# Seven products for eight in a second output projection, and a different block order at its end

## The chip, the cores and the metric

The kernel runs on one core of one Trainium2 chip. The metric is the device time of one execution in microseconds (us). The engines of the core are named as in the profile: PE is TensorE (matrix multiply), PEld its weight loads, DVE is VectorE, ACT is ScalarE, POOL is GpSimd, SP is SyncE, which here only issues DMAs.

## What is computed

Two layers of a decoder trunk work on 256 tokens of 2048 features, in float32. Cut to what matters here:

```
for layer in range(2):
    attn = moba_attention(h, ...) or swa_attention(h, ...)   # ends in  o @ w_o   (256x2048 @ 2048x2048)
    h = layer_norm(ALPHA * h + attn, ln_g[layer, 0], ln_b[layer, 0])
    ffn = conv_ffn(h, w_up, conv_w, conv_b, w_down)          # 2048 -> 2 x 5504 -> 2048
    h = layer_norm(ALPHA * h + ffn, ln_g[layer, 1], ln_b[layer, 1])
```

The change is about `o @ w_o`, the output projection of the attention. "Layer 1" in the title of the change is the first layer, which the code numbers 0; from here on the code's numbers are used, layer 0 and layer 1.

## The kernel before

**Halves.** All weights come through one stream of *halves*: a half is a 128 x 1024 piece (512 KB), that is two weight blocks of 128 rows (`k`) by 512 columns (a *chunk*, `c`). SP issues its load into one of seven `raw` buffers (L143). ACT copies it into the high part `wh` (L162), and DVE subtracts to get the low part `wl` (L171). A product of a data block with a weight block is three matmuls: high by high, high by low, low by high (L386 to L388, or L615 to L617). `take()` hands out the next half and first lets ACT and DVE split three halves further ahead, or more where `reach` says so: near the end of a projection the halves of the next stage go into tiles that have come free (`settle`, `aside`), and the two engines run far ahead of PE.

**Order.** Nothing is scheduled by a tool; the order is that of the program. `step()` counts halves, and `at(n, f)` puts an action `n` steps ahead into an agenda. Each engine works its own instructions in that order, so an action which DVE was given after a split waits for that split, and the split for its weights' DMA.

**The output projection** (`project_out`) has four chunks of 16 blocks. Without quads (layer 0), each chunk has two accumulators, one for each half of the tokens, and after it `fold` adds them to the residual `res` (L521 the first time, L511 later). With quads (layer 1), `two_chunks` does chunks 0 and 1 together: a *quad* is a pair of blocks `2p, 2p+1` in both chunks. Its eight products (two blocks, two chunks, two token tiles) become seven, as in Strassen's scheme. For that it needs sums of weight blocks, made ahead of time in DRAM (the tensors `t`, two halves for each quad, `sum_weights`), and sums of data blocks (`pair_sums`, made by `sum_heads` during the attention). The seven products go into eight accumulator banks; when the quads are done, `chain` combines four of them and `fold` adds the results to `res`.

**Weight sums.** `plan_sums` puts five DMAs for each quad into the agenda: two copies of the plain blocks from DRAM to DRAM on SP (L300), and on POOL one accumulating DMA (L302) and two more (L304, L306), each of which waits for the one before it. The quads of `w_down` (the down projection) are made in the same way during attention and up projection.

**Bias tables.** `spread_bias` writes the relative-position bias of four heads from `ud` to `band` in DRAM; for layer 1 that is on POOL (L317), four DMAs, read by the attention of layer 1 much later.

The order of halves in the two chunks is written out by `wo_halves`: first `WO_LEAD`, then sums (`t`) and plain halves in turn, and at the end `WO_LAST`, two halves of four blocks: blocks 14 and 15 of chunk 0, and then the same of chunk 1.

Of the kernel before, what the change touches and what calls it, by code (L numbers as in the profile page):

```python
# [11 lines left out]
F32 = mybir.dt.float32  # L12
# [5 lines left out]
P = 128  # L18
T = 256
D = 2048  # L20
KB = D // P
NH = 16
# [3 lines left out]
FT = DFF // P  # L26
# [24 lines left out]
TWO_ORDER = [(k, c) for k in range(12) for c in range(2)] + [(k, c) for c in range(2) for k in range(12, KB)]  # L51


QUADS = ((10, 8, 0), (10, 8, 4))
DENSE = ((False, True), (False, False))
LEAD = (4, 2)
WO_LEAD = [(k, 0) for k in range(8, 14)] + [(k, 1) for k in range(8, 12)]
WO_LAST = [(k, c) for c in range(2) for k in (14, 15)]
S_EARLY = 8
QUAD_ORDER = ((0, 1, 2, 3, 4, 5, 8, 9, 6, 7), (0, 1, 2, 3, 4, 5, 6, 7))  # L60
QUAD_LIST = [(l, n, p) for l in range(2) for n in range(3) for p in range(QUADS[l][n])]


def quad_halves(l, n):
# [19 lines left out]
def wo_halves(l):  # L84


    q = range(QUADS[l][2])
    mid = [b for p in q for b in ((2 * p, 0), (2 * p + 1, 0), (2 * p + 1, 1))]
    mid[3:3] = [(12, 1)]
    mid[10:10] = [(13, 1)]  # L90
    halves = lambda bs: [("w", *bs[i:i + 2]) for i in range(0, len(bs), 2)]
    order = halves(WO_LEAD)
    sums, others = [("t", p, i) for p in q for i in range(2)], halves(mid)
    while sums:
        order += [sums.pop(0)] + others[:1]
        others = others[1:]
    return order + others + halves(WO_LAST)

# [6 lines left out]
def trunk(ctx: ExitStack, tc: tile.TileContext, wst, wq, xT_in, x_in, relb, onehot, umask, sinks, conv_in, ln_g, ln_b, out):  # L105
# [114 lines left out]
    def load_input(pool, tables):  # L220
        xc = pool.tile([P, KB, T], F32, name="xc", bufs=1)

        def load_x(k, n=2, queue=nc.sync):
            queue.dma_start(xc[:, k:k + n], xT_in[:, k:k + n, :])

        def split_x(k, n=2):
            ks = slice(k, k + n)
            nc.scalar.activation(xT[:, ks, 0:T], xc[:, ks], AF.Copy)  # L228
            nc.vector.tensor_tensor(out=xT[:, ks, T:2 * T], in0=xc[:, ks], in1=xT[:, ks, 0:T].bitcast(F32),
                                    op=ALU.subtract)  # L230

        load_weights(lambda j: load_x(j, 1, nc.scalar))
        for u in range(1, RAW_FIRST):
            load_weights()
            if u < 3:
                load_x(u + 1, 1)
        load_x(4)
        load_x(6)
        tables()
        split_upto(0, lambda j: split_x(j, 1))  # L240
        for u in range(1, 3):
            split_upto(u)
            split_x(u + 1, 1)
        for k in range(4, KB, 2):
            if k > 6:
                at(k - 7, load_x, k)
            at(k - 3, split_x, k)
        for i in range(RAW_BUFS - RAW_FIRST):
            at(16 + 3 * i, load_weights)

    def load_residual(t):
        nc.sync.dma_start(res[:, t, :], x_in[t * P:(t + 1) * P, :])
# [55 lines left out]
    def plan_sums(quads, n0, step):  # L308


        for j, q in enumerate(quads):
            for i, m in enumerate((0, 2, 5, step + 1, step + 4)):
                at(n0 + j * step + m, sum_weights, q, i)

    def spread_bias(l, h0, h1):
        a = ud[l, h0:h1, :]
# [539 lines left out]
    def layer_attention(l, rest, stage, turnover):  # L856
        oT = st
        kept = []
        if l:
            norm, turned = rest  # L860
            turn, low = turned
            n0 = nexth["i"]
            c = COLS[1]
            norm(c[0])
            norm(c[1])
            split_upto(n0 + 7)
            norm(c[2])

            def early(t, i):
                if t == 0 and i == 5:  # L870
                    pts = [turn(c[j]) for j in range(2)]
                    low(c[0], pts[0])
                    norm(c[3])
                    low(c[1], pts[1])
                if t == 0 and i == 7:
                    low(c[2], turn(c[2]))
                if t == 1 and i == 1:
                    low(c[3], turn(c[3]))
                if t == 1 and i < HALF_BUFS:
                    split_upto(n0 + 8 + i)  # L880

            kept = [acc_tile(), acc_tile()]
            Moving(lambda k: xT[:, k, :], KB).chunk(kept, early=early)
        pool = stage(f"att{l}")
        bias = pool.tile([P, NH, 2 * P], F32, name="bias", bufs=1)
        wo = [(1, 2, p) for p in range(QUADS[1][2])]
        plan_sums(wo[2 * l:2 * l + 2] + [(l, 0, p) for p in range(2)], (54, 2)[l], 10)
        if l == 0:
            load_input(pool, lambda: bias_table(pool))
        else:  # L890
            nc.vector.tensor_scalar(nsk, sk, -1.0, None, op0=ALU.mult)
        for i, h in enumerate(range(0, NH, 4)):
            if l == 0:
                at(8 + 14 * i, spread_bias, l, h, h + 4)
            at((12 + 14 * i, 4 * i)[l], load_bias, bias, l, h, h + 4)

        def v_group(accs=None):
            if not accs:
                accs = [acc_tile(), acc_tile()]
                Moving(lambda k: xT[:, k, :], KB).chunk(accs)  # L900
            return v_evac(accs)

        def v_two_groups():

            accs = [[acc_tile(), acc_tile()] for c in range(2)]
            mv, vts = Moving(lambda k: xT[:, k, :], KB), []
            for k, c in TWO_ORDER:
                wh, wl = mv.block()
                for t in range(2):
                    mv.mm(accs[c][t], k, t, wh, wl)  # L910
                if mv.pos % 2 == 0:
                    step()
                if k == KB - 1:
                    vts.append(v_evac(accs[c]))
            return vts

        def v_evac(accs):
            vt = pool.tile([P, 2, 512], F32, name="vt", bufs=1 if l else 2)

            def evac():  # L920
                for t in range(2):
                    nc.scalar.activation(vt[:, t, :], accs[t], AF.Copy)

            at(0, evac)
            return vt

        places = []

        def wo_sums(p):
            a = places[p // 2][:, p % 2 * 1024:(p % 2 + 1) * 1024]  # L930
            return a[:, 0:512], a[:, 512:]

        def sum_heads(h):

            p = h // 2
            if h % 2 == 0 or p >= QUADS[l][2]:
                return
            if not places:
                places.extend(gbp.tile([P, D], F32R, name=f"gb{i}") for i in range(2))
            w = pool.tile([P, 2 * T + 512], F32, name="fs", bufs=1)  # L940
            for i, step in enumerate(pair_sums(lambda i: oT[:, 2 * p + i, :], w[:, 0:2 * T], w[:, 2 * T:], *wo_sums(p))):
                at(6 + i, step)

        def feat_unit(name, bufs):
            acc = acc_tile()
            ws_unit(acc)
            o = pool.tile([P, T], F32, name=name, bufs=bufs)

            def evac():
                nc.scalar.activation(o, acc[:, T:2 * T], AF.Copy)  # L950
                nc.vector.tensor_tensor(out=o, in0=acc[:, 0:T], in1=o, op=ALU.add)

            at(0, evac, first=True)
            return o

        if l == 0:
            vts = v_two_groups()
            for g in range(NH // 4):
                vt = vts[g] if g < 2 else v_group()
                for j in range(4):  # L960
                    h = 4 * g + j
                    q = feat_unit("qT", 4)
                    k = feat_unit("kT", 4)
                    attention(pool, l, h, q, vt[:, :, j * P:(j + 1) * P], k, bias, oT)
                    sum_heads(h)
        else:
            vt = v_group(kept)
            ks = [feat_unit("kT", KVH) for _ in range(KVH)]
            for h in range(NH):
                q = feat_unit("qT", 4)  # L970
                j = h // GRP
                attention(pool, l, h, q, vt[:, :, j * P:(j + 1) * P], ks[j], bias, oT)
                sum_heads(h)
        return project_out(lambda k: oT[:, k, :], NH, 2 * l, turnover.homes, AF.Gelu_apprx_tanh, turnover,
                           wo_sums=wo_sums if QUADS[l][2] else None)

    class FeedForward:
# [6 lines left out]
        def __call__(self):  # L984
# [3 lines left out]
            self.work = pool.tile([P, 6, T], F32, name="work", bufs=1)  # L988
            self.turn = [0, 0, 0]
            nc.gpsimd.dma_start(self.cw, conv_in[self.l])  # L990
            if self.l == 0:
                for h in range(0, NH, 4):
                    spread_bias(1, h, h + 4)

        def homes(self):
            x, h = ([(tile, j) for j in range(n)] for tile, n in ((xT, SPARE), (self.up, 6)))
# [10 lines left out]
        def run(self, rest):  # L1007
            l, pool = self.l, self.pool
            norm, (turn, low) = rest
            n0 = nexth["i"]  # L1010
# [50 lines left out]
                            at(1, sums, i // 2)  # L1061

            mine = [q for q in QUAD_LIST if q[0] == l and q[1] < 2][2:]
            plan_sums(mine, 12, (4 * FT - 30) // (len(mine) + 3))
            accs = [acc_tile() for _ in range(OPENING)]

            def opened(u):
# [149 lines left out]
```

## Time and profile before

| what | value |
|---|---|
| median of 3 runs (lowest, highest) | 2060.33 us (2060.3, 2060.75) |
| profiled execution: its own time, its span | 2062.13 us, 2060.3 us |
| granted TensorE clock in it | 0.998 |
| busy: PE, PEld, DVE, ACT, POOL | 2052.5, 1772.3, 1568.3, 1064.7, 121.4 us |
| DMA | 520.50 MB, mean 253 GB/s |

Stages as the trace shows them (us from the span's start): layer 0 has its attention to 300, its output projection to 388, the up projection to 871, the down projection to 1090. Layer 1 follows, with its output projection from 1253 to 1343.

In rows of the trace, `out<-in` are the program's tiles, a time in front is the start, the next number the duration in us; `[0.47 <-DVE res L521]` says that the engine had been idle for 0.47 us and that the instruction named ended it. A row of windows gives, for each engine, the busy us and the number of instructions in the stretch.

### The profile page before, as it was taken

Reading aid. Unit: us, or ns where it says so; the run is one execution under the profiler, and the core shown is the slowest. Engines: PE = TensorE matmul, PEld = TensorE weight load, DVE = VectorE, ACT = ScalarE, POOL = GpSimd, SP = SyncE. Lnnn points to the kernel's source line nnn. Section 1 sums busy time; section 2 is a strip of 40 time slices with the busy share of each in tenths; the row PEclk is TensorE's granted clock in tenths of the full one; section 3 lists DMA queues with packets and bytes.
Section 4 is the critical chain, followed back from the end, with each engine's and each line's share of the span. In section 5 each row is a group of like instructions: output and inputs, shape, how many; then the busy total and the mean of one; then the engine's idle time right before and its main releaser. Section 6 shows DMA issues by size and latency. Waiting matters only on the chain.

```text
span 2060.3 us, 29412 instructions
## 1 busy us (share of the span) xinstructions
PE 2052.5 (100%) x10987; PEld 1772.3 (86%) x10987; DVE 1568.3 (76%) x2342; ACT 1064.7 (52%) x1483; POOL 121.4 (6%) x142
## 2 busy tenths in 40 slices
PE   9999999999999999999999999999999999999998
PEld 7888888988888888888888888898888888888886
DVE  5555557698887778787786787988887787887767
ACT  5544446344545545565563556545454545566553
POOL 0000000001111110000000100001111110000000
PEclk9999999999999999999999999999999999999999
DMA  8668888379999995588893977839999997569883
GB/s 320 202 207 261 238 256 290 121 244 293 287 287 304 291 264 192 191 278 307 297 331 131 260 192 223 324 122 286 302 281 305 281 305 213 192 207 318 285 299 117
DMA packets 161553, 520.50 MB, mean 253 GB/s; under 512 B 18640, under 2 KB 23568, under 8 KB 160896
## 3 DMA queue, kind: packets, MB, share of 16 engines
q1 hardware_dynamic: 135488, 469.67, 65.1%
q0 software_dynamic: 25632, 48.68, 15.0%
q8 instruction: 86, 1.41, 0.3%
q14 instruction: 59, 0.48, 0.1%
q10 hardware_dynamic: 288, 0.26, 0.0%
HBM read 516.37 MB, written 90.23 MB: 294 GB/s over the span
## 4 chain that ended last, share of the span: by engine, by line
PE 99%; DMA 0%; DVE 0%; ACT 0%; issue 0%; DVEq 0%; ACTq 0%
PE acc L333 39%; PE acc L336 20%; PE acc L617 5%; PE acc L615 5%; PE acc L616 5%; PE acc L386 5%; PE acc L388 5%; PE acc L387 5%; PE at L617 2%; PE at L615 2%; PE at L616 2%; PE acc L351 1%; PE acc L363 1%; PE at L806 1%; PE at L839 1%; PE at L704 1%
## 5 line engine op out<-in xcount | busy, mean ns | idle before, releaser
L171 DVE TENSOR_TENSOR wl<-raw,wh 128x1024 fp32r<-128x1024 f32 (+1 forms) x724 | 880.6, 1219 | 411.4 <-ACT wh L162 394.3
L162 ACT ACTIVATE wh<-raw 128x1024 fp32r<-128x1024 f32 (+1 forms) x724 | 763.9, 1056 | 714.1 <-PE acc L333 245.4
L333 PE MATMUL acc<-xT,wh 128*128 128x512 f32 x3456 | 872.6, 394 | 0.0
L333 PEld LDWEIGHTS acc<-xT,wh 128*128 128x128 f32 x3456 | 623.5, 189 | 113.0
L336 PEld LDWEIGHTS acc<-xT,wl 128*128 128x128 f32 x3456 | 471.5, 190 | 33.8
L336 PE MATMUL acc<-xT,wl 128*128 128x256 f32 x3456 | 481.9, 282 | 0.0
L615 PE MATMUL acc<-wh,up 128*128 128x512 f32 x328 | 127.6, 389 | 0.0
L616 PE MATMUL acc<-wl,up 128*128 128x512 f32 x328 | 127.6, 389 | 0.0
L617 PE MATMUL acc<-wh,up 128*128 128x512 f32 x328 | 127.6, 389 | 0.0
L1031 DVE SCALAR_TENSOR_TENSOR work<-work,cw 128x255 f32<-128x255 f32 x172 | 83.3, 484 | 6.1
L1032 DVE SCALAR_TENSOR_TENSOR work<-work,cw 128x254 f32<-128x254 f32 x172 | 83.2, 484 | 6.2
L302 POOL DMA_DIRECT2D t<-in_wq_dram x40 | 50.4, 1259 | 446.9 <-DMA t<-in_wq_dram 446.9
L1030 DVE TENSOR_SCALAR work<-work,cw 128x256 f32<-128x256 f32 x172 | 71.1, 413 | 6.2
L1029 DVE TENSOR_TENSOR work<-acc,work 128x256 f32<-128x256 f32 x172 | 71.8, 418 | 1.5 <-ACT work L1028 1.5
L616 PEld LDWEIGHTS acc<-wl,up 128*128 128x128 f32 x328 | 61.6, 188 | 12.8
L617 PEld LDWEIGHTS acc<-wh,up 128*128 128x128 f32 x328 | 61.6, 188 | 12.8
L615 PEld LDWEIGHTS acc<-wh,up 128*128 128x128 f32 x328 | 61.6, 188 | 12.6
L1028 ACT ACTIVATE work<-acc 128x256 f32<-128x256 f32 x172 | 63.3, 368 | 6.5 <-PE acc L363 6.5
L199 ACT ACTIVATE work<-work 128x256 f32<-128x256 f32 x86 | 36.0, 419 | 47.4 <-DVE work L1032 47.4
L304 POOL DMA_DIRECT2D t<-t x40 | 32.9, 824 | 433.0 <-DMA t<-in_wq_dram 389.5
L386 PE MATMUL acc<-wh,xT 128*128 128x512 f32 x144 | 57.6, 400 | 0.2 <-ACT xT L228 0.2
L388 PE MATMUL acc<-wh,xT 128*128 128x512 f32 x144 | 56.4, 392 | 0.0
(252 smaller groups left out, 2189.5 us busy)
## 6 DMA issues: line engine op xcount, KB each, us to landing
raw<-in_wst_dram SPq DMA_DIRECT2D x701, 512.0 KB, 5.4
t<-in_wq_dram SPq DMA_DIRECT2D x80, 512.0 KB, 7.6
raw<-t SPq DMA_DIRECT2D x80, 512.0 KB, 4.5
t<-in_wq_dram POOLq DMA_DIRECT2D x40, 512.0 KB, 11.6
t<-t POOLq DMA_DIRECT2D x80, 256.0 KB, 7.1
gb<-in_ln_g_dram SPq DMA_DIRECT2D x12, 256.0 KB, 5.6
gb<-in_ln_b_dram SPq DMA_DIRECT2D x12, 256.0 KB, 5.2
band<-ud SPq DMA_DIRECT2D x4, 512.0 KB
```

The lines of the kernel that those rows point to most:

```text
L162: nc.scalar.activation(wh[:, c], raws[s][:, c], AF.Copy)
L171: nc.vector.tensor_tensor(out=wl[:, c], in0=raws[s][:, c], in1=wh[:, c].bitcast(F32), op=ALU.subtract)
L333: nc.tensor.matmul(acc, cols(wh, j), xT[:, k, :], start=(k == 0), stop=False)
L336: nc.tensor.matmul(o, cols(wl, j), xT[:, k, 0:T], start=False, stop=(k == KB - 1))
L386: nc.tensor.matmul(acc, sh, wh, start=(k == first), stop=False)
L387: nc.tensor.matmul(acc, sh, wl, start=False, stop=False)
L388: nc.tensor.matmul(acc, sl, wh, start=False, stop=(k == self.nk - 1))
L615: nc.tensor.matmul(bank(key), a[0], wh[:, c], start=key not in begun, stop=False)
L616: nc.tensor.matmul(bank(key), a[0], wl[:, c], start=False, stop=False)
L617: nc.tensor.matmul(bank(key), a[1], wh[:, c], start=False, stop=stop)
L1031: nc.vector.scalar_tensor_tensor(c[:, 1:T], h[:, 0:T - 1], w[:, 1:2], c[:, 1:T], op0=ALU.mult, op1=ALU.add)
L1032: nc.vector.scalar_tensor_tensor(c[:, 2:T], h[:, 0:T - 2], w[:, 0:1], c[:, 2:T], op0=ALU.mult, op1=ALU.add)
```

## The change

`QUADS[0][2]` goes from 0 to 4: layer 0's output projection takes the quad path too. In both layers `WO_LAST` becomes blocks 12 to 15 of chunk 1, and blocks 14 and 15 of chunk 0 move to the middle (`WO_MID`), in place of blocks 12 and 13 of chunk 1. The weight sums of layer 0's four new quads are planned in layer 0's attention from step 18, twelve steps apart, ahead of the first two quads of the down projection; the first two quads of layer 1's output projection, which stood there, move to the end of layer 0's up projection, where the sums stand a little closer. The four `spread_bias` DMAs of layer 1 move from the output projection of layer 0 into its up projection. For layer 0 the scratch of the data sums is a piece of the input tile `xc`.

```diff
-QUADS = ((10, 8, 0), (10, 8, 4))
+QUADS = ((10, 8, 4), (10, 8, 4))
-WO_LAST = [(k, c) for c in range(2) for k in (14, 15)]
+WO_MID = [(14, 0), (15, 0)]
+WO_LAST = [(k, 1) for k in range(12, 16)]
+WO_QUADS = [[(l, 2, p) for p in range(QUADS[l][2])] for l in range(2)]
...
-    mid[3:3] = [(12, 1)]
-    mid[10:10] = [(13, 1)]
+    mid[5:5] = WO_MID[:1]
+    mid[10:10] = WO_MID[1:]
...
+        return xc.rearrange("p k t -> p (k t)")[:, 0:2 * T + 512]
...
-                at(n0 + j * step + m, sum_weights, q, i)
+                at(n0 + int(j * step + m), sum_weights, q, i)
...
-        wo = [(1, 2, p) for p in range(QUADS[1][2])]
-        plan_sums(wo[2 * l:2 * l + 2] + [(l, 0, p) for p in range(2)], (54, 2)[l], 10)
+        spare = None
+        plan_sums(WO_QUADS[l][2 * l:] + [(l, 0, p) for p in range(2)], (18, 2)[l], (12, 10)[l])
         if l == 0:
-            load_input(pool, lambda: bias_table(pool))
+            spare = load_input(pool, lambda: bias_table(pool))
...
-            w = pool.tile([P, 2 * T + 512], F32, name="fs", bufs=1)
+            w = spare if l == 0 else pool.tile([P, 2 * T + 512], F32, name="fs", bufs=1)
...
-            if self.l == 0:
-                for h in range(0, NH, 4):
-                    spread_bias(1, h, h + 4)
...
-            plan_sums(mine, 12, (4 * FT - 30) // (len(mine) + 3))
+            if l == 0:
+                mine += WO_QUADS[1][:2]
+                for i, h in enumerate(range(0, NH, 4)):
+                    at(60 + 16 * i, spread_bias, 1, h, h + 4)
+            plan_sums(mine, 12, (4 * FT - 30) / (len(mine) + 3))
```

With quads, layer 0's `project_out` also loads `gb` (the layer norm's scale and shift) in eight pieces on SP instead of two DMAs on POOL, as layer 1 already did.

## The prediction

> **What bounds the kernel now.** I read the page's busy times first, then its chain, then PE's own waits.
>
> ```profile
> PE   2052.5 (100%) x10987; PEld 1772.3 (86%) x10987; DVE 1568.3 (76%) x2342; ACT 1064.7 (52%) x1483; POOL 121.4 (6%) x142
> ```
>
> ```profile
> PE 99%; DMA 0%; DVE 0%; ACT 0%; issue 0%; DVEq 0%; ACTq 0%
> ```
>
> ```profile
> PE at L261 <- POOL ident masks.py:199: 1.4, 1, 1.4
> PE at L681 <- DVE mr L675: 0.8, 1, 0.8
> PE acc L386 <- DVE res L521: 0.5, 1, 0.5
> PE at L689 <- ACT raw L685: 0.4, 1, 0.4
> PE acc L386 <- ACT xT L228: 0.2, 1, 0.2
> ```
>
> These are all of PE's waits of note: it is busy in 100% of the span, and 99% of the chain that ended last is PE. So time can come from two places only: fewer matmuls, or the one wait among these that this change touches, PE's first L386 behind a `res` fold (L521). The other four are at the start and at the very end of the program, where nothing is edited. And time can be lost only where something new makes PE wait.
>
> **The matmuls that go.** A quad does seven products for eight, a product is three matmuls, and layer 0 gets four quads: 4 x 1 x 3 = 12 matmuls of 512 columns go, and 180 of 192 are left in its first two chunks. The built programs' PE order agrees: 12 matmuls fewer, all in this stage, with the attention's matmuls between the same steps as before. Layer 1 had its quads already and keeps its count. The price of one is read from the quad path of layer 1, its last half and what follows it (PE, in order of time):
>
> ```profile
> 1294.73 0.39 PE L615 MATMUL acc<-up,st 128*128 128x512 f32 x1
> ...
> 1297.22 0.39 PE L617 MATMUL acc<-up,st 128*128 128x512 f32 x1
> 1298.08 0.47 PE L386 MATMUL acc<-up,st 128*128 128x512 f32 x1 [0.47 <-DVE res L521]
> ```
>
> The durations of 0.39 overlap; what counts is from start to start. The half has 12 matmuls, so 11 steps from 1294.73 to 1297.22: 2.49 / 11 = 0.226 us each. Twelve are worth 12 x 0.226 = 2.72 us, on the path. The Trainium skill, in TensorE: Matmul & The Clock Gate, section Back-to-back issue gap, has about 131 ns for such a matmul in a stream of weight loads and matmuls; by that the saving would be 12 x 0.131 = 1.57 us. This trace disagrees (0.226 us), and the sum goes by the trace.
>
> **The wait at the end of the two chunks.** In the same rows the next chunk starts 1298.08 - 1297.22 = 0.86 us after the last matmul, where 0.23 is the pace: 0.63 us are lost in layer 1. DVE shows why:
>
> ```profile
> 1292.27 5.06 DVE L171 TENSOR_TENSOR wl<-raw,wh 128x1024 fp32r<-128x1024 f32 x4
> 1297.25 1.28 DVE L521 SCALAR_TENSOR_TENSOR res<-res,acc 128x512 f32<-128x512 f32 x2
> 1298.45 0.68 DVE L602 TENSOR_TENSOR work<-at,work 128x512 f32<-128x512 f32 x1
> ```
>
> The two folds that free chunk 0's banks came only after four splits of halves far ahead, paced by their DMAs. Chunk 0's last product was in the half before the last (blocks 14 and 15), whose matmuls end where the half above begins, at 1294.73; the folds were given to DVE after the split of the stage's 28th half. After the change the last product of chunk 0 is a sum half, one half earlier, and in the built order of DVE the two folds stand after the 26th split, in both layers. Two of the four splits thus come behind the folds: these can start at about 1292.27 + 5.06 / 2 = 1294.8 and end 1.28 later, at 1296.1, and PE wants the banks at 1297.45. There are 1.4 us to spare, so the 0.63 us go, and what is late next is nothing: the two splits that slip by some 2.6 us belong to the fifth and sixth half of the next chunk, which PE reaches four and five halves of 2.7 us later. Layer 0 now has this same stage, so I take a wait of 0 there, with 0.63 as the other end.
>
> **The added work and what covers it.** Layer 0 has six more halves to load and split, and four data sums. Prices:
>
> ```profile
> L171 DVE TENSOR_TENSOR wl<-raw,wh 128x1024 fp32r<-128x1024 f32 (+1 forms) x724 | 880.6, 1219 | 411.4 <-ACT wh L162 394.3
> L162 ACT ACTIVATE wh<-raw 128x1024 fp32r<-128x1024 f32 (+1 forms) x724 | 763.9, 1056 | 714.1 <-PE acc L333 245.4
> ```
>
> ```profile
> L437 DVE TENSOR_TENSOR fs<-fs x12: 282/284/292, 1177.8 to 1221.8; 128x128 f32<-128x128 f32 x12
> L454 DVE TENSOR_TENSOR fs<-st x8: 414/418/420, 1175.1 to 1218.8; 128x256 f32<-128x256 f32 x8
> L437 DVE TENSOR_TENSOR gb<-fs,gb x4: 680/681/681, 1182.3 to 1225.7; 128x512 fp32r<-128x512 f32 x4
> ```
>
> Splits: 6 x 1.22 = 7.3 us of DVE and 6 x 1.06 = 6.3 us of ACT. A data sum is 2 x 0.42 + 4 x 0.28 + 0.68 = 2.6 us of DVE, 10.6 us for four, spread over 100 us of attention. Four more combinations and folds of 0.68 (the L602 row) are 5.4 us. Off the path: DVE is 76% busy, and a quad half takes PE 6 x 0.226 = 1.36 us against DVE's 1.22. That cover is thin, but layer 1 runs the same stage with PE's only wait the one above. Were it gone, six halves would cost PE up to 6 x (1.22 + 1.06) = 13.7 us, split against product in turn.
>
> The weight sums of layer 0's own quads need to be there when SP comes to load them, since a late one holds SP's queue and every weight load behind it.
>
> ```profile
> L300 SPq DMA_DIRECT2D t<-in_wq_dram x8: 496/497/606, 172.2 to 267.2; - x8
> ```
>
> ```profile
> 179.91 1.08 POOL L302 DMA_DIRECT2D t<-in_wq_dram  x1 [157.21 <-DMA t<-in_wq_dram]
> ...
> 197.47 0.81 POOL L306 DMA_DIRECT2D t<-t  x1 [4.90 <-DMA t<-t]
> ```
>
> Before, the first sum stood at step 54, and its DMAs ran from 172 to 197 us. The new plan has the fourth and last of layer 0's quads at this same step 54, so all are done soon after 200 us, about 100 us before the projection starts at 300. The three earlier ones fall into a stretch with room:
>
> ```profile
> core 0: us, PE busy (x) PEld busy (x) DVE busy (x) ACT busy (x) POOL busy (x), PEclk, DMA share, GB/s
> 50.00:150.00 100.00, 100.00 (x584) 88.45 (x583) 59.39 (x103) 50.17 (x90) 0.00 (x0) 1.00 0.61 202
> ```
>
> Cost nothing: the DMA engines are 0.61 busy there. The eight `gb` pieces on SP wait for the last quad's matmuls, as in layer 1, where PE did not wait for them; the `gb` and `spread_bias` DMAs that leave POOL in this stage give nothing back, since no PE wait stands there.
>
> **The up projection of layer 0** gets two more quads and four `spread_bias`, where the DMA engines are full already:
>
> ```profile
> 450.00:750.00 300.00, 300.00 (x1719) 263.92 (x1717) 244.72 (x401) 150.65 (x215) 37.99 (x42) 1.00 1.00 291
> 750.00:870.00 120.00, 120.00 (x689) 105.63 (x688) 96.54 (x153) 60.52 (x86) 3.53 (x4) 1.00 0.64 201
> ```
>
> ```profile
> 434.67 1.12 POOL L302 DMA_DIRECT2D t<-in_wq_dram  x1 [81.54 <-DMA t<-in_wq_dram]
> ...
> 768.01 0.81 POOL L306 DMA_DIRECT2D t<-t  x1 [5.29 <-DMA t<-t]
> ```
>
> ```profile
> 314.39 1.12 POOL L317 DMA_DIRECT2D band<-ud  x1 [0.26 <-issue]
> ...
> 352.07 1.06 POOL L317 DMA_DIRECT2D band<-ud  x1 [10.88 <-issue]
> ```
>
> POOL goes from DMA to DMA: 16 quads in 768.01 - 434.67 = 333 us, 20.8 each. Four `spread_bias` took (352.07 - 314.39) / 3 = 12.6 us each. Put into that chain, two quads and four of these make it 2 x 20.8 + 4 x 12.6 = 92 us longer: it ends at about 860, and the engines stay full through the stretch where they were 0.64 busy, but not into the down projection at 871. Behind the waiting POOL stand only more sums. All those that the down projection needs come before layer 1's two. So PE pays only if a weight load comes late:
>
> ```profile
>   issue: 106.8, 73
>   PE acc L333: 54.1, 73
>   ACT work L1028: 1.2, 2
> ```
>
> ```profile
> DMA to landing us min/median/max: 3.1/6.4/12.2
> ```
>
> The first are all reasons why ACT's splits waited from 410 to 860: none is a DMA. The second is the weight loads' landing there. A half takes PE 300 / 1719 x 16 = 2.79 us. With seven buffers a load is issued 7 x 2.79 - 1.06 - 1.22 = 17.2 us ahead of its split, and the split stands 3 x 2.79 - 1.06 - 1.22 = 6.1 us ahead of PE: PE waits only if a load takes over 23.3 us. The longest took 12.2. I take 0; the other end is in the rivals.
>
> **The sum.** 2.72 + 0.63 = 3.35 us less. For the profiled execution: span 2060.3 to 2056.9, its own time 2062.13 to 2058.8; its span is the median of the runs to 0.03 us, so the median goes from 2060.33 to about 2056.9. That is 0.16%. About 0.2%, or 4.1 us, is what a measurement of this kernel can tell from no change, so this counts as within.
>
> **Rivals.** *The folds are late again.* In layer 1 the wait stays: 2.72 us less, 2057.6. If layer 0's new stage has it too: 2.72 - 0.63 = 2.1 less, 2058.2. For it: the folds still stand behind 26 splits that DMAs pace, and 1.4 us is one split's worth. Against: two splits fewer and one half of PE more, both read from rows.
>
> *Slower: weight loads of the up projection queue behind `spread_bias`.* How long those took to land:
>
> ```profile
> DMA to landing us min/median/max: 11.2/12.7/14.9
> ```
>
> If one is served wholly ahead of the weights when these take their longest, a load needs 12.2 + 12.7 = 24.9 us, or 12.2 + 14.9 = 27.1: 1.6 to 3.8 us over the cover, four times. That is 6.4 to 15.2 us, so 2063.3 to 2072.1. It decides from (3.35 + 4.1) / 4 = 1.9 us each, a landing of 25.2 us. For it: a share of 1.00. Against: POOL's accumulating DMAs are in flight all along there, and the longest load is half of what it takes. The Trainium skill, in DMA: Bandwidth & Descriptors, section Queues, rings and completion order, says that each DMA engine goes round between its queues packet by packet, so that POOL's queue could not be served wholly first; the longest landing of 12.2 us beside POOL's traffic agrees.
>
> *A sum of layer 0's quads, or its splits, come late:* as bounded above, up to 13.7 us, so 2056.9 + 13.7 = 2070.6; against it, layer 1's own stage.
>
> *More than forecast:* under 2056.2, 0.8 us beyond the sum. It would have to come from a hold-up that shows as PE work, whose ends are modelled; the runs' scatter of 0.45 us adds to it.
>
> **How the numbers follow.** Forecast 0.69; more than forecast 0.15; folds late 0.09; late weight loads 0.05; late sums or splits 0.02. Faster by over 0.2% is 0.15, slower 0.07, within 0.69 + 0.09 = 0.78. The range goes down to 2055.7, half a microsecond into the faster case, which takes half of it, and up to 2059.0: the late folds, or one slow load at 1.6 us (2058.5), with the scatter. Left out are about 0.08 below and 0.07 above.
>
> **What would show it.** Right: 12 matmuls fewer in layer 0's projection; no PE wait behind L521's line in either layer, with the folds ending over 1 us before the next chunk; POOL's sums ending near 860; no split in the up projection that waits for a DMA. Wrong: a gap in PE at the end of the two chunks, a weight load of over 20 us in the up projection of layer 0, or SP held by a load from `t` ahead of layer 0's projection.

## The result and the profile after

| | before | after |
|---|---|---|
| median (lowest to highest, 22 runs each) | 2060.61 us (2060.17 to 2062.03) | 2057.54 us (2057.0 to 2058.54) |
| after over before | | 0.9985, 95% interval 0.9979 to 0.9991 |
| profiled execution: span, own time | 2060.3, 2062.13 us | 2055.3, 2057.03 us |

The medians differ by 3.07 us, the forecast was 3.35. It is a small gain, within 0.2% as forecast; the whole interval lies below 1. The profiled executions differ by 5.0 us, and that is more than the change brought, as will be seen. One run of all those below, among the 11 of experiment 4, took 2237.58 us at a mean granted clock of 0.85; it shifts that median by 0.01 us.

The page after, busy times and chain, answers to the first lines of before:

```profile
PE 2048.0 (100%) x10975; PEld 1770.4 (86%) x10975; DVE 1588.5 (77%) x2384; ACT 1073.4 (52%) x1494; POOL 131.4 (6%) x152
...
PE 100%; DVE 0%; ACT 0%; issue 0%; POOL 0%; DVEq 0%; POOLq 0%
```

PE has 10987 - 10975 = 12 matmuls fewer, and is the whole chain still; DVE got 20 us and POOL 10 us more work, which nobody waits for. PE's own waits after:

```profile
PE at L264 <- POOL ident masks.py:199: 1.4, 1, 1.4
PE at L684 <- DVE mr L678: 0.8, 1, 0.8
PE at L692 <- ACT raw L688: 0.4, 1, 0.4
```

The wait for the folds of `res` is not among them any more, in either layer.

Where the time came from is read by setting the same instruction of both PE timelines side by side. First before (the last matmuls of layer 0's attention; the first of layer 0's up projection; the first matmul of layer 1's output projection; the first of its up projection; the last six matmuls of the program), then after:

```profile
286.80 0.59 PE L839 MATMUL at<-PT,vt 128*128 128x256 f32 x2
...
388.19 1.00 PE L351 MATMUL acc<-xT,wh 128*128 128x256 f32 x7
...
1253.09 0.48 PE L615 MATMUL acc<-wh,st 128*128 128x512 f32 x1
...
1343.60 1.60 PE L351 MATMUL acc<-xT,wh 128*128 128x256 f32 x12
...
2051.26 4.52 PE L689 MATMUL at<-work,raw 2*128 2x512 f32 x6 [0.41 <-ACT raw L685]
```

```profile
286.70 0.59 PE L842 MATMUL at<-PT,vt 128*128 128x256 f32 x2
...
385.38 3.88 PE L354 MATMUL acc<-xT,wh 128*128 128x256 f32 x31
...
1250.28 0.48 PE L618 MATMUL acc<-wh,st 128*128 128x512 f32 x1
...
1340.04 4.00 PE L354 MATMUL acc<-xT,wh 128*128 128x256 f32 x32
...
2047.70 2.84 PE L692 MATMUL at<-work,raw 2*128 2x512 f32 x6 [0.42 <-ACT raw L688]
```

After is ahead by 0.10 us, then 2.81, 2.81, 3.56 and 3.56. So 2.71 us were gained in layer 0's output projection, nothing from there through the up and down projections and layer 1's attention, 0.75 in layer 1's output projection, and nothing up to the last six matmuls: 3.46 us by the change. The 0.10 ahead of it came before any edited PE work: it arises in PE's first 20 us, and in the other profiles this early part lies anywhere from 0.43 behind before to 0.24 ahead, so it is taken off in each comparison below. The profiles of experiments 4, 8 and 9, read in the same way, give 2.72 and 0.75 us again (0.74 in 9). The last six matmuls took 1.68 us less (4.52 to 2.84), and the change does not touch them: they are the same six instructions, at another clock (the windows that hold most of them, before and then after):

```profile
2051.00:2055.00 4.00, 3.74 (x6) 1.42 (x6) 2.31 (x4) 1.54 (x4) 0.00 (x0) 0.66 0.34 133
```

```profile
2047.00:2051.00 4.00, 3.11 (x7) 1.11 (x7) 3.11 (x6) 1.87 (x4) 0.00 (x0) 0.94 0.31 120
```

The granted clock was 0.66 before and 0.94 after. This part comes and goes from run to run: the profile of experiment 4 below had 4.76 us there again. It is seen in the times too. Each run of the two kernels has a mean granted clock, 0.999 or 0.998. After had 12 runs at 0.999 with a median of 2057.26, and 10 at 0.998 with 2058.09. Of the 62 runs of before that went beside the experiments, 46 were at 0.999 (median 2060.74) and 16 at 0.998 (2061.75). At equal clock the two kernels are 3.5 and 3.7 us apart, close to the 3.46 of PE's rows. That the medians show less fits the 10 of 22 runs of after at the lower clock, where before had 16 of 62; the clocks of the 22 runs of before in the table are not on record.

Now the ends of the two chunks after, PE and DVE, layer 1:

```profile
1294.41 0.39 PE L620 MATMUL acc<-up,st 128*128 128x512 f32 x1
1294.64 0.39 PE L389 MATMUL acc<-up,st 128*128 128x512 f32 x1
```

```profile
1289.79 2.51 DVE L173 TENSOR_TENSOR wl<-raw,wh 128x1024 fp32r<-128x1024 f32 x2 [0.19 <-ACT wh L164]
1292.21 1.28 DVE L524 SCALAR_TENSOR_TENSOR res<-res,acc 128x512 f32<-128x512 f32 x2
```

and layer 0:

```profile
339.75 0.39 PE L620 MATMUL acc<-up,st 128*128 128x512 f32 x1
339.98 0.39 PE L389 MATMUL acc<-up,st 128*128 128x512 f32 x1
```

```profile
336.02 2.49 DVE L173 TENSOR_TENSOR wl<-raw,wh 128x1024 fp32r<-128x1024 f32 x2 [1.44 <-ACT wh L164]
338.43 1.28 DVE L524 SCALAR_TENSOR_TENSOR res<-res,acc 128x512 f32<-128x512 f32 x2
```

In both layers PE goes on at its pace of 0.23 us. The folds end at 1292.21 + 1.28 = 1293.49 in layer 1, 1.15 us before PE needs the banks; in layer 0 at 339.71, with 0.27 us to spare.

### The profile page after: what moved, and what is told of

The parts are those of the page before. It is cut to its first block, busy times and chain, and to the rows that moved or that the text cites. A ratio compares the mean times of both kernels' runs of the same rounds, so it can differ in the third digit from the quotient of the medians.

```text
span 2055.3 us, 29510 instructions
## 1 busy us (share of the span) xinstructions
PE 2048.0 (100%) x10975; PEld 1770.4 (86%) x10975; DVE 1588.5 (77%) x2384; ACT 1073.4 (52%) x1494; POOL 131.4 (6%) x152
## 4 chain that ended last, share of the span: by engine, by line
PE 100%; DVE 0%; ACT 0%; issue 0%; POOL 0%; DVEq 0%; POOLq 0%
PE acc L336 39%; PE acc L339 20%; PE acc L620 6%; PE acc L618 6%; PE acc L619 6%; PE acc L389 4%; PE acc L391 4%; PE acc L390 4%; PE at L620 2%; PE at L619 2%; PE at L618 2%; PE acc L354 1%; PE acc L366 1%; PE at L809 1%; PE at L842 1%; PE at L707 1%
## 5 line engine op out<-in xcount | busy, mean ns | idle before, releaser
L620 PEld LDWEIGHTS acc<-wh,up 128*128 128x128 f32 x328 | 61.6, 188 | 12.7
L618 PEld LDWEIGHTS acc<-wh,up 128*128 128x128 f32 x328 | 61.6, 188 | 12.7
L619 PEld LDWEIGHTS acc<-wl,up 128*128 128x128 f32 x328 | 61.6, 188 | 12.7
L307 POOL DMA_DIRECT2D t<-t x44 | 36.5, 829 | 480.6 <-DMA t<-in_wq_dram 468.2
```

Source lines behind the costliest of these rows:

```text
L618: nc.tensor.matmul(bank(key), a[0], wh[:, c], start=key not in begun, stop=False)
L619: nc.tensor.matmul(bank(key), a[0], wl[:, c], start=False, stop=False)
L620: nc.tensor.matmul(bank(key), a[1], wh[:, c], start=False, stop=stop)
```

## The experiments

**Theory.** The gain is two separate terms: 12 matmuls less in layer 0, and the fold wait of layer 1, which goes because the folds stand behind fewer splits on DVE. **Rivals.** The wait goes because chunk 0's last product is taken earlier on PE. Layer 0's quads would have done without the new order. And for the up projection: the `spread_bias` DMAs do delay weight loads there and only happen to be hidden. Times are medians, with the kernel before run beside them.

**1: the new order alone**, layer 0 without quads.

```diff
 # before, with
-WO_LAST = [(k, c) for c in range(2) for k in (14, 15)]
+WO_MID = [(14, 0), (15, 0)]
+WO_LAST = [(k, 1) for k in range(12, 16)]
...
-    mid[3:3] = [(12, 1)]
-    mid[10:10] = [(13, 1)]
+    mid[5:5] = WO_MID[:1]
+    mid[10:10] = WO_MID[1:]
```

> The kernel before with the new block order alone (blocks 12 to 15 of chunk 1 last), no quads in layer 0. My theory, that the folds stood behind too many splits on DVE: they now stand after the 26th split of layer 1's stage, the PE wait at its end goes, and from there on PE starts everything 0.63 to 0.75 us earlier than before; layer 0 unchanged; 2060.6 to about 2059.9. Rival, that the wait came from something else at the change of chunks (the new accumulator, the first half of the next chunk): the gap of 0.86 us stays and the time with it.

Measured: 2060.06 us (11 runs) beside 2060.92 (33 runs); ratio 0.9995, interval 0.9986 to 1.0004. The times alone don't tell this from no change; PE's timeline does. Set against before it is 0.31 us behind from 18 us on, ahead of any edited work, and stays so up to layer 1's output projection; from there on it is 0.44 ahead. So 0.75 us are gained, all at this place, and the place of the wait looks so:

```profile
1297.54 0.39 PE L618 MATMUL acc<-up,st 128*128 128x512 f32 x1
1297.76 0.39 PE L387 MATMUL acc<-up,st 128*128 128x512 f32 x1
```

0.22 us from matmul to matmul where before had 0.86. The second term is worth 0.75 us and stands by itself.

**2: the quads alone**, after with the old order.

```diff
 # after, with
-WO_MID = [(14, 0), (15, 0)]
-WO_LAST = [(k, 1) for k in range(12, 16)]
+WO_LAST = [(k, c) for c in range(2) for k in (14, 15)]
...
-    mid[5:5] = WO_MID[:1]
-    mid[10:10] = WO_MID[1:]
+    mid[3:3] = [(12, 1)]
+    mid[10:10] = [(13, 1)]
```

> The changed kernel with the old block order: layer 0 has its four quads, but the last two halves are blocks 14 and 15 of chunk 0 and then of chunk 1, so that the folds stand after 28 splits in both layers. My theory: the 12 matmuls are gone (2.72 us) and both layers have a PE wait of about 0.6 to 0.75 us at the end of the two chunks; against the kernel before 2.72 - 0.7 = 2.0 us less, about 2058.6. Rival, that layer 0's stage differs (no heads of layer 1's pace ahead of it): no wait in layer 0, 2.7 less, about 2057.9.

Measured: 2059.92 us (11 runs) beside 2060.92; ratio 0.9997, interval 0.9989 to 1.0006. PE's wait for the folds is back, now in both layers (the waits, then PE in layer 0 and in layer 1):

```profile
PE acc L388 <- DVE res L523: 1.6, 2, 1.1
```

```profile
340.26 0.39 PE L619 MATMUL acc<-up,st 128*128 128x512 f32 x1
341.76 0.47 PE L388 MATMUL acc<-up,st 128*128 128x512 f32 x1 [1.11 <-DVE res L523]
...
1296.31 0.39 PE L619 MATMUL acc<-up,st 128*128 128x512 f32 x1
1297.18 0.47 PE L388 MATMUL acc<-up,st 128*128 128x512 f32 x1 [0.48 <-DVE res L523]
```

The hole in layer 0 is 341.76 - 340.26 = 1.50 us, where layer 1 has 0.87 and the pace is 0.23. Against before, PE is 1.33 us ahead after layer 0's projection instead of 2.72, so 1.39 of the 2.72 are lost again. The expectation had about 0.7 for layer 0's wait and so 2.0 us less than before in all; the wait is twice that, and the medians are 1.0 apart. The two edits belong together: in layer 0 the quads are worth half without the order.

**3: fewer splits ahead of the folds, in the old order.** `reach` grows more slowly in a projection with quads, so that the folds come after 26 splits instead of 28, while chunk 0's last product stays in the half before the last.

```diff
 # before, with
-                reach[i] = i + min(AHEAD + (i - first) * 3 // 5, len(ring) - 1)
+                slope = (i - first) * (1 if wo_sums else 3) // (3 if wo_sums else 5)
+                reach[i] = i + min(AHEAD + slope, len(ring) - 1)
```

> The kernel before, its block order as it was, but in layer 1's output projection the splits run ahead more slowly (one more half in three instead of three in five), so that the folds stand after the 26th split and not the 28th. It tells two readings of the wait apart. Theory: the folds were late because of the splits ahead of them on DVE; the wait goes though chunk 0's last product is as late as before, PE 0.63 to 0.75 us earlier from there, about 2059.9. Rival: they were late because chunk 0's last product ends only one half before the next chunk; the gap of 0.86 us stays, 2060.6.

Measured: 2060.25 us (11 runs) beside 2060.92; ratio 0.9997, interval 0.9988 to 1.0006. Again the timeline decides. DVE and PE at the end of layer 1's two chunks:

```profile
1292.39 2.52 DVE L171 TENSOR_TENSOR wl<-raw,wh 128x1024 fp32r<-128x1024 f32 x2
1294.82 1.28 DVE L522 SCALAR_TENSOR_TENSOR res<-res,acc 128x512 f32<-128x512 f32 x2
```

```profile
1297.53 0.39 PE L618 MATMUL acc<-up,st 128*128 128x512 f32 x1
1297.76 0.39 PE L386 MATMUL acc<-up,st 128*128 128x512 f32 x1
```

No wait, and PE goes from 0.31 us behind before to 0.44 ahead at this place, a gain of 0.75 as in 1. The last product of chunk 0 was as late as before; it is the splits put ahead of the folds that cost the 0.75 us, and not the product's place on PE. That rival falls. So the new order is read as working by the same step: it makes the program give DVE the folds two splits sooner.

**4: `spread_bias` doubled** in layer 0's up projection.

```diff
 # after, with
                     at(60 + 16 * i, spread_bias, 1, h, h + 4)
+                    at(60 + 16 * i, spread_bias, 1, h, h + 4)
```

> The changed kernel, with each of the four table DMAs (spread_bias) in layer 0's up projection issued twice in a row: it doubles the suspected load where the DMA engines are full. Theory: weight loads have 23.3 us before PE waits, the longest with four tables took 15.8; with eight I expect 16 to 22 and no PE wait, POOL's sums of this stage ending at 850 to 880 instead of 832, and the time as in the changed kernel, 2057.5 within 0.7. Rival, late weight loads: landings over 23.3 us, PE waits behind ACT or DVE splits between 550 and 750 us, 1.6 to 3.8 us for each of four places, so 2060 or more.

Measured: 2057.67 us (11 runs) beside 2060.92; ratio 0.9984, interval 0.9975 to 0.9993, as after. No wait of PE lies between 405 and 900 us. The longest weight load from 410 to 860 landed after 14.2 us; the expectation had 16 to 22, and after had 15.8. The last new sum goes out at 877.44 (POOL), within the 850 to 880 expected and already in the down projection, and nothing there waits for it:

```profile
860.15 1.33 POOL L305 DMA_DIRECT2D t<-in_wq_dram  x1
...
877.44 0.81 POOL L309 DMA_DIRECT2D t<-t  x1 [5.34 <-DMA t<-t]
```

Twice the number of tables is hidden too. But the second of a pair went out only when the first had landed:

```profile
650.30 1.10 POOL L320 DMA_DIRECT2D band<-ud  x1 [16.07 <-DMA band<-ud]
```

So this run doubles the time in which tables are on their way, not the load at any one moment, and a hidden delay would look the same. The cover was taken away next.

**5: four `raw` buffers instead of seven; 6: the same, with `spread_bias` back in the output projection; 7: five buffers.** One run of each, so without a spread.

```diff
 # 5: after, with
-RAW_BUFS = 7
+RAW_BUFS = 4
 # 6: as 5, and in the output projection
             nc.gpsimd.dma_start(self.cw, conv_in[self.l])
+            if self.l == 0:
+                for h in range(0, NH, 4):
+                    spread_bias(1, h, h + 4)
...
                 mine += WO_QUADS[1][:2]
-                for i, h in enumerate(range(0, NH, 4)):
-                    at(60 + 16 * i, spread_bias, 1, h, h + 4)
 # 7: after, with
-RAW_BUFS = 7
+RAW_BUFS = 5
```

> The changed kernel with four raw buffers for weights instead of seven. It measures the cover that the prediction worked out: 4 x 2.79 - 2.28 = 8.9 us from a load's issue to its split and 6.1 more to PE, 15.0 in all instead of 23.3. If this reckoning is right, ACT's splits wait for DMAs in layer 0's up projection wherever a landing takes over 8.9 us, and PE waits there for at most about a microsecond, where a landing is over 15 us (the longest was 15.8). If the cover is less than worked out, PE waits at many places between 450 and 830 us. The projections, which take a half in 1.4 us, get slower by several us in either case; they are not what this run is for.

> Four raw buffers as in the run before, and the four table DMAs (spread_bias) back in layer 0's output projection, where the kernel before had them; the two more quads stay in the up projection. With four buffers PE waited six times there, 9.3 us, from 580 to 760 us, and not at all in layer 1's up projection, which has no tables. If the tables cause the late loads, the waits in layer 0's up projection go (0 to 1 us are left). If the two more quads and their closer spacing cause them, they stay at 5 us or more.

> The changed kernel with five raw buffers. The prediction's reckoning gives a cover of 5 x 2.79 - 2.28 + 6.1 = 17.8 us, the longest landing with seven buffers was 15.8: no PE wait in layer 0's up projection. But with four buffers a longest landing of 15.1 cost up to 3.7 us at once where the reckoning gave 0.1, so the cover may be some 4 us less than reckoned: then one or two waits of 1 to 2 us appear at the places of the tables.

Measured: 2106.49, 2107.95 and 2066.44 us. The totals say little here, since the fewer buffers cost waits in other stages as well; the up projection of layer 0 is what counts (PE's waits from 405 to 900 us of 5, and the landing of weight loads from 400 to 880 in 5, 6 and 7):

```profile
PE acc L336 <- ACT wh L164: 9.3, 6, 3.7
```

```profile
DMA to landing us min/median/max: 3.1/6.9/15.1
```

```profile
DMA to landing us min/median/max: 3.1/6.5/11.0
```

```profile
DMA to landing us min/median/max: 3.1/7.6/12.9
```

In 5 PE waited six times for late loads, in 6 not once in that window, and the longest landing fell from 15.1 to 11.0 us. The only edit between the two is where the tables are spread, and in 5 some 8.4 of the 9.3 us were waited for loads that had been issued while a table was on its way. So they do delay weight loads, as the rival said, and seven buffers hide it. In 6 the waits went to the stage that got the tables back (300 to 404 us):

```profile
PE acc L389 <- DVE res L524: 6.9, 1, 6.9
PE at L707 <- DVE res L650: 4.1, 1, 4.1
```

where 5 had 4.8 and 1.2 us. By the prediction's formula four buffers give 4 x 2.79 - 2.28 + 6.1 = 15.0 us of cover. A longest landing of 15.1 should have cost 0.1 us once; measured are 9.3 us in six waits. The longest wait, 3.7 us, was for a load that landed 14.4 us after its issue, and one of 1.6 us (at 764.93) for a load of 10.0. Landing less wait is the cover that there was: 10.7 and 8.4 us here, up to 12.2 at the others. So the cover is some 4 us less than the formula has it at the longest wait, and 3 to 7 less over all. A likely reason is that the lead of the splits over PE was used up before the slowest load came: ACT's splits had waited for loads four times from 678 to 686 us. No run tests that. Five buffers (17.8 by the formula, about 14 less those 4) had no such wait at 12.9 us.

**8: longer filler at the very end.** `finish` fills PE's wait for the last statistics with 12 small transposes (`STILL`); here 20.

```diff
 # after, with
-STILL = 12
+STILL = 20
```

> The changed kernel with 20 instead of 12 idle transposes at the very end, where PE waits for the last token's statistics. In the profile before the granted clock fell to 0.53 in the last stretch and the last six matmuls took 4.52 us, in the profile after it was 0.92 and they took 2.84. Theory, that the clock falls because PE stands still for about 0.8 us before them: PE stays busy, the six take 2.6 to 2.9 us in every run, runs lie at the lower end of the changed kernel's 2057.0 to 2058.5, median about 2057.0. Rival, that the fall does not follow from this gap: spread and median as in the changed kernel, about 2057.5.

Measured: 2057.36 us (11 runs, 2056.96 to 2057.64) beside 2060.74 (14 runs); ratio 0.9983, interval 0.9973 to 0.9992. PE's 0.8 us wait at L684 is filled and no longer a wait. That gains nothing directly, as PE goes on when DVE is done. The last six matmuls took 2.84 us in this profile, and the median is not the 2057.0 expected.

**9: experiments 3 and 8 on after**, with the slower run-ahead in both layers.

```diff
 # after, with
-STILL = 12
+STILL = 20
...
-                reach[i] = i + min(AHEAD + (i - first) * 3 // 5, len(ring) - 1)
+                slope = (i - first) * (1 if wo_sums else 3) // (3 if wo_sums else 5)
+                reach[i] = i + min(AHEAD + slope, len(ring) - 1)
```

> The changed kernel with 20 idle transposes at the very end and with the slower run-ahead of the splits in both output projections: the folds stand after the 25th split instead of the 26th. The time between the end of the folds and the next chunk's first matmul, 0.28 us in layer 0 and 1.15 in layer 1 after the change, should grow by about one split's pace of 1.28 us; the time itself should not change, since PE does not wait there: median as with 20 transposes alone, 2057.4 within 0.3. Rival, that splits which come later cost PE a wait further on: slower than 2057.7, with a PE wait in the third or fourth chunk.

Measured: 2057.34 us (11 runs, 2056.91 to 2057.74) beside 2060.86 (15 runs); ratio 0.9982, interval 0.9973 to 0.9991. The folds now end 0.63 us ahead of need in layer 0 and 2.79 in layer 1, and it gives nothing, since nothing waited. In layer 0 that is 0.36 more than in after, not the 1.28 expected: DVE stood idle for 1.67 us there, waiting for ACT's last split ahead of the folds. All 22 runs of 8 and 9 had a mean clock of 0.999, where 6 of the 29 runs of before beside them had 0.998. That speaks for the longer filler, but the profile of 9 speaks against a full remedy:

```profile
2047.69 3.62 PE L693 MATMUL at<-work,raw 2*128 2x512 f32 x6 [0.42 <-ACT raw L689]
```

3.62 us for the six matmuls, between the 2.84 and the 4.52 above, although 8's expectation had them short in every run. Neither version is measurably faster than after (0.2 us less, with ranges that overlap).

## Why the prediction was right, point by point

**Twelve matmuls, 2.72 us: right.** 2.71 us by the rows above, all in layer 0's projection. The 0.226 us of this trace held. By the 131 ns that the Trainium skill gives in TensorE: Matmul & The Clock Gate, section Back-to-back issue gap, it would have been 1.57 us, an estimate; the measurement differs, and decides.

**Layer 1's wait, 0.63 us: right in cause, small in size.** It was 0.75. The prediction priced the hole alone. The matmul after a hole also takes longer: in before and in 2 it lasts 0.47 us instead of 0.39, and the next one starts 0.30 us behind it, where the pace is 0.23. That makes 0.70 or 0.71; the rest is spread over the matmuls that follow.

**Wait of 0 in layer 0's new stage: right, with less room than said.** The prediction gave both layers 1.4 us; measured are 1.15 and 0.27. DVE stood idle there for 1.44 us ahead of 336.02, because ACT's split ahead of it waited for its load (ACT, layer 0, then the same split in layer 1):

```profile
334.92 1.06 ACT L164 ACTIVATE wh<-raw 128x1024 fp32r<-128x1024 f32 x1 [1.62 <-DMA raw<-in_wst_dram]
```

```profile
1288.69 1.06 ACT L164 ACTIVATE wh<-raw 128x1024 fp32r<-128x1024 f32 x1 [0.35 <-PE at L620]
```

The two layers' stages lie 1294.64 - 339.98 = 954.66 us apart on PE, so this split came 0.9 us later in layer 0. Its load was issued as early, measured against PE (327.80 and 1282.46). What held them up is not shown; the DMA share was 0.78 in this stage and 0.75 in layer 1's, and no run separated the causes. The other end of the term, 0.63, would have been too small for this layer: with the old order it is 1.39 (experiment 2).

**The weight sums of layer 0: right.** They are ready soon after 200 us (POOL):

```profile
196.03 0.82 POOL L309 DMA_DIRECT2D t<-t  x1 [5.64 <-DMA t<-t]
```

and the price is a fuller stretch, a DMA share of 0.84 where it was 0.61 (windows of after):

```profile
50.00:150.00 100.00, 100.00 (x584) 88.49 (x582) 65.02 (x123) 51.28 (x92) 6.43 (x7) 1.00 0.84 254
```

**POOL's chain to about 860: too long.** It ended 28 us sooner (its first and last row):

```profile
432.44 1.06 POOL L305 DMA_DIRECT2D t<-in_wq_dram  x1 [118.35 <-DMA t<-in_wq_dram]
...
832.01 0.81 POOL L309 DMA_DIRECT2D t<-t  x1 [5.97 <-DMA t<-t]
```

Of those 399.6 us, 18 quads at 20.8 are 374; the four `spread_bias` added 25, so 6.3 each and not 12.6. The price of 12.6 was read from four tables that stood back to back, and there each went out when the one before it had landed: their distance is about their time to landing (median 12.7 us), and experiment 4 shows that wait by name. Here one table stands between two sums, and POOL goes on without waiting for its landing (the first went out at 559.11 and landed after over 15 us; the next sum went out at 569.89). What it adds lies in its issue (1.2 to 1.9 us) and in slower sums beside it: the step from L307 to L309 beside the first table took 14.2 us, where it took 7.0 and 8.8 in the two quads before.

**No weight load late in the up projection: right by a smaller margin.** Landing of the tables, and then of the weights from 410 to 860 us, after:

```profile
DMA to landing us min/median/max: 15.7/20.0/24.3
```

```profile
DMA to landing us min/median/max: 3.2/7.5/15.8
```

Before these were at most 14.9 and 12.2. Both got slower, which fits engines that both share, neither served wholly ahead of the other. The Trainium skill, in DMA: Bandwidth & Descriptors, section Queues, rings and completion order, has each engine alternate between its queues packet by packet, and these two rows agree. The rival's price of 12.2 + 12.7 = 24.9 us was never reached. But the cover is not 23.3 either: if seven buffers lose the 4 us that four lost at the longest wait of experiment 5, it is about 19, an estimate, and some 3 us are left instead of 8. The mechanism of the slower rival was real; its point of decision was probably put too far off.

**The sum and its base.** 3.35 was forecast, 3.46 is what PE's rows give, and the medians differ by 3.07. The median after came out 0.64 us above the forecast: 0.28 of it is the base (2060.33 was the median of three runs, and 22 runs had 2060.61), another 0.28 the smaller difference, and the rest rounding. That the profiled span equalled the median to 0.03 us was chance: a run's own time lies 1.7 to 1.8 us above its span (2062.13 and 2060.3; 2057.03 and 2055.3), and the profiled run of before had the lower clock at its end. For the same reason the profiled span came out at 2055.3 where 2056.9 was forecast: the last six matmuls alone took 1.68 us less.

**The signs.** The matmul count, the missing waits and the splits of the up projection that wait for no DMA came as named. Two did not: the folds end over 1 us before the next chunk in layer 1 alone, and POOL's sums ended at 832 and not near 860.

## What to carry to other kernels

When an engine works in program order, what you run ahead on it also stands ahead of the short step that frees the next stage's buffers; look at what was given to that engine just before the step, not only at when its inputs are ready. Subtract two traces at the same instruction in several places, and take off what they differ by ahead of the first edit, instead of comparing spans: the change was worth 3.46 us where spans differed by 5.0, mostly because the program's last matmuls went at another clock. A transfer that is hidden is best tested by thinning its cover until it shows, since doubling it showed nothing here.

## What was not expected of the hardware

The same six last matmuls took from 2.84 to 4.76 us in these profiles, with a granted clock of 0.94 in after and 0.66 in before, behind a stretch in which PE was idle for parts of a microsecond only.

The traces' clock records show what sets the time of the six. In the profiles of before, after and experiments 1 to 4, 8 and 9 the clock goes from 1.00 to 0.50 once near the end. It did so 0.8 us after the start of the six in 4 (they took 4.76 us), 1.0 in before (4.52), 1.4 in 3 (4.11), 1.9 in 9 (3.62), and 2.7 us or more in 1, 2, after and 8 (2.84 in all four). The stretch at full clock ahead of the fall had lasted 2048.00 us in four of these profiles and 2044.58 in the other four, 600 and 599 times 3.413 us; it began 4.1 to 7.0 us from the span's start. In experiment 5 the clock also fell for 3.41 us shortly after PE's wait of 3.7 us. So the clock seems to change on a grid of 3.41 us that starts at another moment of the program in each run. The Trainium skill, in TensorE: Matmul & The Clock Gate, section What's actually happening, tells of a free-running window of about 3.4 us, which these lengths agree with. In before PE was idle for only 1.2 us (0.77 and 0.41) of the last 3.41 ahead of the fall; what in this stretch made the clock fall is not shown.

The longer filler did not keep the clock up: it fell in the profiles of 8 and 9 too, in 8 only after the six had ended. Why all 22 runs of 8 and 9 had the higher mean clock stays open. By the medians at each mean clock the end of the program makes 0.8 us (after) to 1.0 us (before) from one run to another, a quarter or more of what this change is worth.
